# Down projection's partial sums: copied by ScalarE and added by GpSimd's accumulating DMAs, in place of VectorE's adds

## The chip, the cores and the metric

The kernel runs on one core of a Trainium2 chip. A core has TensorE (PE, matrix products into PSUM), VectorE (DVE), ScalarE (ACT), GpSimd (POOL) and SyncE (SP, which issues most DMAs); each takes its own instructions strictly in order, and they wait for one another by semaphores. The metric is the time of one execution on the device, in microseconds, and of several runs the median.

## The reference

One layer of a streaming encoder: state-space heads and latent attention heads, side by side, and then a dense SwiGLU block, for 512 prompt tokens and 64 later tokens that share the weights. The change lies in the SwiGLU block:

```python
hf = rmsnorm(x, p['norm_ffn'])
x = x + (jax.nn.silu(hf @ p['w_gate']) * (hf @ p['w_up'])) @ p['w_down']
```

`x` has 576 tokens of 1024 channels, `w_gate` and `w_up` are 1024 x 2816 and `w_down` is 2816 x 1024, all float32. In the kernel the block is followed by a norm of each token (the gain `norm_final` and the outputs `y`).

## The kernel before

The tokens lie along the free dimension: the residual `x2` is eight tiles `x2[t]` of 128 channels x 576 tokens, four of which share one buffer (`x2t[0]`, `x2t[1]`; both are called `x` in the profile). A float32 product is made of three products of rounded parts: high by high, high by low, low by high. `split_weights` makes the parts of a weight tile: ScalarE copies it into the rounded type (line 112, `wh_...`), VectorE subtracts that from the original (line 113, `wl_...`).

The hidden 2816 channels are 22 tiles `f`. For each, `gu_weights(f)` loads 2 x 512 KB of gate and up weights and forms the sums of a seven-product scheme (lines 806 to 820), and `gu_steps(f)` multiplies them in seven steps m1 to m7 into PSUM banks `ps_x`, `ps_y`, `ps_z`; some steps add onto a bank that an engine has read in between (`onto=True`). ScalarE and VectorE gather the results in `g` and `u` (lines 914 to 939), and `finish` makes `silu(g) * u` and splits it into `prod[f]` (`pr` in the profile). The tile `f = 0` has a form of its own, `gu_first`: there the norm's factor `R2` and its inverse form `Ri` (part of `fz`) are computed, and `g` is multiplied by `R2` (line 894).

The factor `R2` is put on `g` alone and left out of `u`, so that the down projection's sums lack it. In its place the residual is multiplied by `Ri`, the inverse of `R2`, once, in the first call of `down` (line 965); the norm that follows the block takes the common scale out again.

`down(fs)` is the down projection of a group of hidden tiles. The groups are `f` = 0 to 4, 5 to 9, 10 to 13, 14 to 17; the last, 18 to 21, goes through the closing code. `down` of a group is called after the first tile of the next group. For each of eight output tiles `t` and each half of the tokens (288) it makes 15 or 12 matmuls of 128 x 288 into one PSUM bank (`ps_d`; line 953), and VectorE adds the bank to the residual (line 966). Banks come from three sets in turn: `hm` has two, `sc` and `pp` three each, and `ps_x` (`sc`) and `ps_y`, `ps_z` (`pp`) use the latter two as well.

The temporaries `g`, `u` and others come from `tmp`, a ring of seven buffers of 128 x 582 floats with one tag: a new one waits until what last read its buffer is done.

The closing code multiplies the last group in two parts of the tokens (lines 953 and 1005: `add`), sums the squares (on ScalarE, VectorE and GpSimd), normalises and sends the output.

What order instructions take on an engine is decided in three ways. A planner orders all that isn't fixed, by a model of durations that it has. The table `ISSUE` fixes, for each engine, a sequence of instructions by their number in the order in which the code makes them; it covers the whole of the first part of the kernel and, with its last lines, some instructions of the SwiGLU block. And the closing part is written in its order by hand (`manual_schedule`).

Of the kernel before, what the change touches and what calls it, by code (L numbers as in the profile page):

```python
# [14 lines left out]
ALU = mybir.AluOpType  # L15
# [39 lines left out]
def hybrid_layer_kernel(ctx: ExitStack, tc: tile.TileContext, a, o):  # L55
    nc = tc.nc
    pe, act, dve, pool, sp = nc.tensor, nc.scalar, nc.vector, nc.gpsimd, nc.sync
# [58 lines left out]
    def weights(src, n, name):  # L116

        raw = wslot(wpool, f"wr_{name}")
        sp.dma_start(raw[:, :n], src)
        return split_weights(raw[:, :n], name)  # L120
# [12 lines left out]
    def wk(w, k, m=P):  # L133
        return tuple(z[:, k * m : (k + 1) * m] for z in w)
# [30 lines left out]
    def norm_steps(R, src, n, view=lambda z: z, eps=True):  # L165

        w = R.shape[1] if len(R.shape) == 2 else T
        y0, nv, u = (view(tmp(f"nr_{z}", w)) for z in "yvu")

        def first():  # L170
            act.activation(y0, src, AF.Ln, scale=1.0 / n, bias=epsb if eps else 0.0)
            dve.tensor_scalar(nv, src, -0.5 / n, -0.5 * EPS if eps else 0.0, ALU.mult, ALU.add)
            act.activation(y0, y0, AF.Exp, scale=-0.5)
            act.activation(u, y0, AF.Square)

        def second():
            dve.tensor_tensor(u, u, nv, ALU.mult)
            dve.scalar_tensor_tensor(R, u, 1.5, y0, ALU.add, ALU.mult)

        return first, second, nv  # L180
# [115 lines left out]
    for hf in range(2):  # L296
        cols = slice(hf * TH, (hf + 1) * TH)
# [441 lines left out]
    cat_y, x2, x2t = [], [], []  # L739
# [117 lines left out]
    def fbank(tag, name):  # L857
        return bank(tag, name)[:, :TH]
# [87 lines left out]
    def down_terms(fs, t):  # L946
        w = weights(a["w_down"][t][:, fs[0] * P : (fs[-1] + 1) * P], len(fs) * P, f"d{fs[0]}_{t}")
        return [(wk(w, k), prod[f]) for k, f in enumerate(fs)]

    def down_half(ps, terms, cols, first=True, last=True):  # L950
        for k, ((whi, wlo), (xhi, xlo)) in enumerate(terms):
            for i, (w, x) in enumerate(((whi, xhi), (whi, xlo), (wlo, xhi))):
                pe.matmul(  # L953
                    ps, w, x[:, cols], start=first and k == 0 and i == 0, stop=last and k == len(terms) - 1 and i == 2,
                )

    def down(fs):

        for t in range(KT):
            terms = down_terms(fs, t)  # L960
            for hf, cols in enumerate(HC):
                ps = fbank(("hm", "sc", "pp")[(2 * t + hf) % 3], f"ps_d{fs[0]}_{t}")
                down_half(ps, terms, cols)
                if fs[0] == 0:
                    dve.tensor_tensor(x2[t][:, cols], x2[t][:, cols], Ri[:, cols], ALU.mult)
                dve.tensor_tensor(x2[t][:, cols], ps, x2[t][:, cols], ALU.add)  # L966

    CUTS = (0, 5, 10, 14, LAST, FT)
    PARTS = tuple(range(i, j) for i, j in zip(CUTS, CUTS[1:]))
# [2 lines left out]
    for part in PARTS:  # L972
        for f in part:
            if f:
                first, rest, middle = gu_steps(f)
                for step in (first, *late, *middle):
                    step()
                late = rest
            if f == part[0] and f:
                for step in late:  # L980
                    step()
                late = ()
                down(prev)
        prev = part
# [15 lines left out]
    def lbank(tag, name, i):  # L1000
        return bank(tag, name)[:, : parts[i].stop - parts[i].start]
# [30 lines left out]
    ps = [lbank(tag, f"ps_l0_{t}", 0) for t, tag in enumerate(("hm", "hm", "sc", "pp"))]  # L1032
# [36 lines left out]
    with tc.manual_schedule(engines={pe.engine, dve.engine, pool.engine, act.engine}):  # L1069
        pn0, pn1 = lbank("sc", "ps_n3_0", 0), bank("pp", "ps_n3_1")[:, : len(BL)]  # L1070
        first, second, _ = norm_steps(pn0, pn0, D, eps=False)
# [32 lines left out]
        first, second, _ = norm_steps(Rt, pn1, D, eps=False)  # L1104
# [32 lines left out]
def issue_in_order(tc, nc):  # L1137
# [48 lines left out]
405 395 391 396 398 394 392 400 399 401 403 402 420 406 404 408 407 409 412 410 417 414 411 413 418 462 416 421 423  # L1186
419 464 425 422 424 415 433 431 426 432 429 428 427 438 430 434 469 463 436 435 437 439 442 441 443 466 440 444 451
465 446 467-468 452-453 445 447 455 454 448 473 475 456 477 476 474 457 472 470 478 458 449 479 488 459 490 485 492
480 489 491 471 450 503 481 505 493-494 482 460 495 487 500 507 504 496 506 518 461 508 502 510 568 575 545 509 512
483 525 511 497 520 519 501 522 486 484 573 521 515 513 517 548 523-524 570 498 530 537-538 527 543 516 526 565 499  # L1190
542 528 555 540 560 514 529 532 553 547 552 557 533 562 541 539 534 550 577 558 531 563 579 578 544 580 535
""",
    "ACT": """
0-5 8 6-7 10 9 13 11 14 12 15 17-18 16 21 19 24 20 23 40 22 25 44 26-27 51 28-33 48-49 55 34-35 37 36 59 50 41-42
# [6 lines left out]
230 237 236 271 231 244 235 247 238 245 248-251 246 256 254 260 253 261 255 258 262 257 264 252 266 265 263 267-268  # L1201
277 269 259 272-276 283 279-281 284 286 282 278 292 285 290 287 289 288 301 291 293 295 294 297 299 296 300 302-303
298 308 304-305 309 306 311 328 307 310 315-316 312-314 329 317 330 318-319 331 335 320-324 332 336 334 333 325 337
339 338 344-345 342 346 343 326 347-348 353-355 352 351 327 356-357 362 340 363 360 358 341 361 364-366 349 373-374
350 359 375 370 367 369 368 376-378 371 379-380
""",
    "POOL": """
0-3 7 18 28 4 8 5 9 6 10 26 11 27 12 29 13-17 20-23 19 24-25 31 30 32-42 53 55 57 59 54 56 58 60 43-52 61-73
""",
    "SP": """  # L1210
11-14 16 15 17-20 23 22 25 21 24 31 26 32 39-40 36 33 38 41-42 37 43-47 55 77 62 79 54 56 58 63 81 57 60 59 61 68 66
# [102 lines left out]
```

## Time and profile before

| what | us |
|---|---|
| median of 3 runs | 654.88 (653.42 to 655.2) |
| span of the profiled execution, first to last instruction | 651.7 |
| matmuls of the four down projections ahead of the closing code (line 953, `ps_d`) | 314.5 to 581.9 |
| last gate and up matmul onto `ps_x` (line 852) | 618.2 |
| the 64 adds of line 966 | 327.5 to 583.3 |
| VectorE busy in the whole span | 512.4 |
| ScalarE busy in the whole span | 339.3 |

The profile counts instructions and busy time of each engine. A matmul of 128 x 288 is listed with some 0.295 us because it overlaps the next; their number in a stretch tells the pace. "Idle before" is time in which an engine stood still ahead of an instruction, with what ended it. In a timeline, the columns are the start, the duration, the engine, the line, the operation, what is written from what, and the number of like instructions that were merged.

### The profile page before, as it was taken

The numbers are of one execution on the slowest core, as the hardware profiler recorded it, in microseconds if no ns is written. First come the engines' busy times: TensorE is split into PE (matmuls) and PEld (weight loads), VectorE is DVE, ScalarE is ACT, GpSimd is POOL, SyncE is SP. The second block draws the span as 40 slices with busy tenths as digits, with TensorE's granted clock in tenths as the row PEclk, the third lists the DMA queues.
The fourth block names the chain that finished last, engine by engine and source line by source line (L and its number), as shares of the span: only waits on it lengthen the run. The fifth ranks groups of instructions, "written<-read, shape, count | busy, mean of one in ns | idle before, by whom it ended". The sixth has DMA issues, their size and how long they took to land.

```text
span 651.7 us, 11921 instructions
## 1 busy us (share of the span) xinstructions
PE 639.9 (98%) x4731; PEld 611.8 (94%) x4731; DVE 512.4 (79%) x935; ACT 339.3 (52%) x630; POOL 41.3 (6%) x80
## 2 busy tenths in 40 slices
PE   9999999998999999999999999999999999999995
PEld 8898989885787899999999999999999999999995
DVE  6899987899776699999996776775768577876655
ACT  7645426769674567665523445223533345334364
POOL 1321104001010000000000000000000000000023
PEclk9999999999999999999999999999999999999998
DMA  8312375323220232133422233311232224222004
GB/s 314 127 62 70 93 171 143 113 66 129 86 76 33 99 102 92 65 109 103 131 80 97 79 101 101 110 66 65 81 114 98 98 66 128 68 98 98 2 1 145
DMA packets 26151, 63.22 MB, mean 97 GB/s; under 512 B 3418, under 2 KB 10088, under 8 KB 25840
## 3 DMA queue, kind: packets, MB, share of 16 engines
q1 hardware_dynamic: 24560, 60.77, 28.3%
q0 software_dynamic: 816, 1.13, 0.8%
q8 instruction: 37, 0.61, 0.4%
q10 hardware_dynamic: 720, 0.57, 0.3%
q14 instruction: 18, 0.15, 0.1%
HBM read 58.03 MB, written 3.30 MB: 94 GB/s over the span
## 4 chain that ended last, share of the span: by engine, by line
PE 84%; DVE 3%; ACT 1%; DMA 1%; issue 1%; POOL 0%; POOLq 0%; DVEq 0%; ACTq 0%
PE ps_x L852 21%; PE ps_d L953 18%; PE ps_z L852 10%; PE ps_o L443 8%; PE ps_y L852 5%; PE ps_in L128 4%; PE ps_z L443 3%; PE ps_l L953 3%; PE ps_p L852 2%; PE sc L657 2%; PE pv L704 1%; PE ptp L679 1%; PE ps_v L590 1%; PE ps_q L443 1%; PE ps_y L527 1%
## 5 line engine op out<-in xcount | busy, mean ns | idle before, releaser
L953 PE MATMUL ps_d<-pr,wh_d 128*128 128x288 f32 x576 | 115.4, 294 | 0.0
L852 PE MATMUL ps_x<-xop,wh_gu_S 128*128 128x288 f32 x504 | 101.8, 295 | 0.0
L953 PEld LDWEIGHTS ps_d<-pr,wh_d 128*128 128x128 f32 x576 | 92.5, 188 | 0.0
L953 PE MATMUL ps_d<-pr,wl_d 128*128 128x288 f32 x288 | 84.6, 295 | 0.0
L852 PEld LDWEIGHTS ps_x<-xop,wh_gu_S 128*128 128x128 f32 x504 | 80.6, 188 | 0.2
L113 DVE TENSOR_TENSOR wl_gu_S<-gu,wh_gu_S 128x1024 fp32r<-128x1024 f32 x44 | 53.6, 1224 | 34.4 <-PE ps_y L852 13.8
L852 PE MATMUL ps_x<-xop,wl_gu_S 128*128 128x288 f32 x252 | 73.4, 295 | 0.0
L112 ACT CAST wh_gu_S<-gu 128x1024 fp32r<-128x1024 f32 x44 | 46.3, 1052 | 48.4 <-PE ps_d L953 25.4
L953 PEld LDWEIGHTS ps_d<-pr,wl_d 128*128 128x128 f32 x288 | 54.0, 188 | 0.0
L852 PEld LDWEIGHTS ps_x<-xop,wl_gu_S 128*128 128x128 f32 x252 | 47.0, 188 | 0.0
L128 PE MATMUL ps_in<-xs,wh_in 128*128 128x288 f32 x256 | 45.2, 298 | 1.2 <-DVE sp_a L351 1.0
L112 ACT CAST wh_d<-wr_d 128x640 fp32r<-128x640 f32 (+1 forms) x32 | 21.5, 673 | 39.1 <-PE ps_x L852 14.8
L128 PEld LDWEIGHTS ps_in<-xs,wh_in 128*128 128x128 f32 x256 | 37.5, 188 | 2.3 <-ACT up L381 1.2
L852 PE MATMUL ps_z<-xop,gu_a 128*128 128x288 f32 x252 | 38.0, 296 | 0.0
L852 PE MATMUL ps_z<-xop,wh_gu_S 128*128 128x288 f32 x168 | 36.0, 296 | 0.0
L852 PE MATMUL ps_x<-xop,wh_gu_A 128*128 128x288 f32 x168 | 35.3, 298 | 0.0
L852 PEld LDWEIGHTS ps_z<-xop,gu_a 128*128 128x128 f32 x252 | 35.1, 188 | 0.0
L852 PE MATMUL ps_y<-xop,wh_gu_A 128*128 128x288 f32 x168 | 34.2, 294 | 0.0
L966 DVE TENSOR_TENSOR x<-ps_d,x 128x288 f32<-128x288 f32 x64 | 28.8, 453 | 6.7 <-PE ps_d L953 6.5
L112 ACT CAST wh_gu_A<-gu 128x1024 fp32r<-128x1024 f32 x22 | 23.1, 1049 | 17.5 <-PE ps_d L953 11.5
L113 DVE TENSOR_TENSOR wl_gu_A<-gu,wh_gu_A 128x1024 fp32r<-128x1024 f32 x22 | 26.9, 1223 | 5.2 <-PE ps_x L852 3.9
L1049 POOL TENSOR_TENSOR fz<-fz,sq 128x320 f32<-128x320 f32 x3 | 2.6, 880 | 445.3 <-ACT sq L1044 445.3
(339 smaller groups left out, 1643.7 us busy)
## 6 DMA issues: line engine op xcount, KB each, us to landing
gu<-in_w_gu SPq DMA_DIRECT2D x44, 512.0 KB, 3.7
wr_d<-in_w_down SPq DMA_DIRECT2D x16, 320.0 KB, 2.9
wr_in<-in_w_in SPq DMA_DIRECT2D x8, 512.0 KB, 4.0
wr_out<-in_w_out SPq DMA_DIRECT2D x8, 512.0 KB, 3.2
wr_d<-in_w_down SPq DMA_DIRECT2D x16, 256.0 KB, 2.7
cumb<-cumD SPq DMA_DIRECT2D x5, 512.0 KB, 4.6
x<-in_xT SPq DMA_DIRECT2D x2, 1152.0 KB, 7.5
wr_z<-in_w_in SPq DMA_DIRECT2D x4, 512.0 KB, 4.4
```

The source lines that it names most:

```text
L112: act.copy(hi, raw)
L113: dve.tensor_tensor(lo, raw, hi.bitcast(F32), ALU.subtract)
L128: pe.matmul(ps[:m, hf, :n], w, x[:, hf * n : (hf + 1) * n], start=start and k == 0 and i == 0, stop=stop and k == last and i == 2,)
L443: pe.matmul(ps[:, :n], w, x[:, cols], start=k == 0 and i == 0, stop=k == len(terms) - 1 and i == 2,)
L527: pe.matmul(py[64 * j : 64 * j + 64, p * P : p * P + L], xdt[:L, h * HD : (h + 1) * HD], wts[:L, h, :L], start=True, stop=True,)
L590: pe.matmul(ps[:n], l, r, start=j == 0, stop=j == 2)
L657: pe.matmul(s[:, :nk], qs[:, j, q0 : q0 + P], ks[:, j, :nk], start=True, stop=True)
L679: pe.transpose(pp[:, k : k + P], prs[p, i][:, j, b * P : b * P + P], ident)
L704: pe.matmul(pv[64 * j : 64 * j + 64, b * P :], V[b][:, h * HD : (h + 1) * HD], pts[p, b, j], start=b == 0, stop=True, skip_group_check=b > 0,)
L852: pe.matmul(ps, p, q, start=not onto and first and kp == kps[0] and j == 0, stop=onto or (last and kp == kps[-1] and j == 2), skip_group_c ...
L953: pe.matmul(ps, w, x[:, cols], start=first and k == 0 and i == 0, stop=last and k == len(terms) - 1 and i == 2,)
L966: dve.tensor_tensor(x2[t][:, cols], ps, x2[t][:, cols], ALU.add)
```

## The change

In `down`, a tile `dn` is taken from the ring of temporaries for each output tile. ScalarE copies each half of the sum from PSUM into it, and a DMA of GpSimd's queue adds `dn` to `x2[t]` with `accum_op` (128 x 576 floats, 288 KB). There are 64 copies and 32 DMAs. The multiplications by `Ri` in the first call remain on VectorE. The numbers in `ISSUE` are adapted where instructions were added or went; it no longer fixes the place of some of them.

```diff
         for t in range(KT):
             terms = down_terms(fs, t)
+            dn = tmp(f"dn{fs[0]}_{t}")
             for hf, cols in enumerate(HC):
                 ps = fbank(("hm", "sc", "pp")[(2 * t + hf) % 3], f"ps_d{fs[0]}_{t}")
                 down_half(ps, terms, cols)
                 if fs[0] == 0:
                     dve.tensor_tensor(x2[t][:, cols], x2[t][:, cols], Ri[:, cols], ALU.mult)
-                dve.tensor_tensor(x2[t][:, cols], ps, x2[t][:, cols], ALU.add)
+                act.copy(dn[:, cols], ps)
+            pool.dma_start(x2[t], dn, accum_op=ALU.add)
...
     "DVE": """
...
-480 489 491 471 450 503 481 505 493-494 482 460 495 487 500 507 504 496 506 518 461 508 502 510 568 575 545 509 512
-483 525 511 497 520 519 501 522 486 484 573 521 515 513 517 548 523-524 570 498 530 537-538 527 543 516 526 565 499
-542 528 555 540 560 514 529 532 553 547 552 557 533 562 541 539 534 550 577 558 531 563 579 578 544 580 535
+480 489 491 471 450 503 481 505 493-494 482 460 495 487 500 507 504 496 506 518 461 508 502 510 556 509 512 483 525
+511 497 520 519 501 522 486 484 559 521 515 513 517 544 523-524 498 530 537-538 527 541 516 526 499 540 528 514 529
+532 547 543 546 549 533 552 539 534 561 550 531 553 563 562 564 535
...
     "ACT": """
...
-339 338 344-345 342 346 343 326 347-348 353-355 352 351 327 356-357 362 340 363 360 358 341 361 364-366 349 373-374
-350 359 375 370 367 369 368 376-378 371 379-380
+339 338 344-345 342 346 343 326 347-348 353-355 352 351 327 356-357 362 340 363 360 358 341 361 364-366 349 373 376
+350 359 379 370 367 369 368 382 385 388 371 391 394
...
     "POOL": """
-0-3 7 18 28 4 8 5 9 6 10 26 11 27 12 29 13-17 20-23 19 24-25 31 30 32-42 53 55 57 59 54 56 58 60 43-52 61-73
+0-3 7 18 28 4 8 5 9 6 10 26 11 27 12 29 13-17 20-23 19 24-25 31 30 32-42 53 55 57 59 54 56 58 60 43-52 61-68 101-105
```

## The prediction

> **What bounds the kernel now.** I read the page first, then the chain of waits, then windows over the second half, where every line of the change lies.
>
> ```profile
> span 651.7 us, 11921 instructions
> PE 639.9 (98%) x4731; PEld 611.8 (94%) x4731; DVE 512.4 (79%) x935; ACT 339.3 (52%) x630; POOL 41.3 (6%) x80
> ...
> PE 84%; DVE 3%; ACT 1%; DMA 1%; issue 1%; POOL 0%; POOLq 0%; DVEq 0%; ACTq 0%
> ```
>
> TensorE carries 84% of the chain, VectorE 3%. But a busy PE is not yet a PE at its peak, so the windows, which count matmuls:
>
> ```profile
> core 0: us, PE busy (x) PEld busy (x) DVE busy (x) ACT busy (x) POOL busy (x), PEclk, DMA share, GB/s
> 280.00:285.00 5.00, 5.00 (x40) 5.00 (x39) 5.00 (x8) 3.25 (x6) 0.00 (x0) 1.00 0.54 188
> 285.00:290.00 5.00, 5.00 (x40) 5.00 (x39) 5.00 (x9) 4.06 (x6) 0.00 (x0) 1.00 0.00 0
> 290.00:295.00 5.00, 5.00 (x40) 5.00 (x39) 5.00 (x10) 2.22 (x5) 0.00 (x0) 1.00 0.62 206
> 295.00:300.00 5.00, 5.00 (x40) 5.00 (x39) 5.00 (x10) 1.57 (x2) 0.00 (x0) 1.00 0.19 57
> 320.00:365.00 45.00, 45.00 (x342) 45.00 (x341) 32.75 (x57) 13.97 (x20) 0.00 (x0) 1.00 0.27 94
> 410.00:450.00 40.00, 40.00 (x303) 40.00 (x303) 27.16 (x45) 12.37 (x18) 0.00 (x0) 1.00 0.22 76
> 485.00:520.00 35.00, 35.00 (x266) 35.00 (x265) 27.41 (x47) 13.03 (x18) 0.00 (x0) 1.00 0.23 83
> 550.00:585.00 35.00, 35.00 (x266) 35.00 (x265) 27.66 (x48) 13.45 (x20) 0.00 (x0) 1.00 0.28 97
> 585.00:620.00 35.00, 35.00 (x263) 35.00 (x262) 20.57 (x30) 15.27 (x22) 0.00 (x0) 1.00 0.16 55
> ```
>
> The rows from 320 to 585 hold the four down projections. Each has 7.6 matmuls a microsecond (342 in 45, 266 in 35) at a granted clock of 1.00: 0.132 us each, the same in all of them. TensorE waits for nothing there, so work taken from VectorE buys nothing. VectorE is 68 to 79% busy there, but in the four rows from 280 to 300 it has no gap at all, while TensorE still runs at full pace. Whatever VectorE gets extra in that stretch is late for somebody.
>
> **What goes from VectorE, and what ScalarE gets.** 64 adds go, 64 copies of the same shape come.
>
> ```profile
> L966 DVE TENSOR_TENSOR x<-ps_d,x x64: 447/453/458, 327.5 to 583.3; 128x288 f32<-128x288 f32 x64
> ...
> L914 ACT COPY g<-ps_x 128x288 f32<-128x288 f32 x16 | 6.4, 399 | 8.2 <-PE ps_x L852 8.2
> ```
>
> Removed: 64 x 0.453 = 29 us of VectorE, worth 0 by the rows above. Added: 64 x 0.399 = 25.5 us of ScalarE, 6.4 in each projection. Between 485 and 520 ScalarE goes from 13.0 to 19.4 busy of 35, so it keeps up. A copy ends the use of a PSUM bank. In the built program the tightest of these banks is wanted again 61 matmuls after its sum is done, 61 x 0.132 = 8.0 us, against 0.4 for the copy and about 1.05 for a weight cast ahead of it: cost 0. Without that cover each copy would cost its 0.4. The order of TensorE's instructions is the same in both built programs, and so are the distances of the weight splits from their matmuls (24 matmuls, 3.2 us, at the least after 320). Bounds here: 0 to 1 us.
>
> **The accumulating DMAs.** 32 of 288 KB, on a queue that has nothing else to do between the last head copies and the closing sums, so nothing is queued behind them there.
>
> ```profile
> q1 hardware_dynamic: 24560, 60.77, 28.3%
> ...
> qs<-rrp POOLq DMA_DIRECT2D x16, 36.0 KB, 4.4
> ...
> out_ckvT<-ckf POOLq DMA_DIRECT2D x1, 288.0 KB, 2.5
> ...
> gu<-in_w_gu SPq DMA_DIRECT2D x44, 512.0 KB, 3.7
> ```
>
> No row shows an accumulating DMA. Nearest is a plain one of the same shape and queue, 2.5 us to landing; the slowest kind on that queue took 4.4. I take 5 us as an estimate (2.5 doubled, for the second operand that is read), with 2.5 and 9.4 (5.0 plus those 4.4) as its ends. What waits: the `dn` tiles share seven buffers with `g` and `u`, and ScalarE, in order, waits for a landing before it writes a reused one. In the two later projections the copy of tile 5 waits for the DMA of tile 0, 120 matmuls = 15.8 us earlier; the waits of the next `g` and `u` come so much later that the n-th of the eight DMAs may land n x 6.9 us after the first copy at the tightest (n = 8: 420 matmuls). Behind the waiting copy stand the casts of the next gate and up weights, and TensorE behind them with 24 matmuls to spare. At 5 us: cost 0. Load on the engines: q1 moved 60.77 MB in 0.283 x 651.7 = 184 us of all sixteen, so 0.295 MB is 0.9 us and twice that 1.8, per tile of 24 matmuls (3.2 us): a share of 0.56 on top of 0.28, below 1, and weights that land in 3.7 have some 60 matmuls (8 us) between their issue and use: 0. SP's loads keep their places. At the end, the last accumulate is issued near 583 and the next read of the residual is long after:
>
> ```profile
> L1005 DVE TENSOR_TENSOR x<-ps_l,x x16: 414/454/492, 625.7 to 641.7; 128x320 f32<-128x320 f32 x8, 128x256 f32<-128x256 f32 x8
> ```
>
> 42 us for one landing: 0.
>
> The Trainium skill, "Collectives: The Full Stack", section "The bandwidth ceiling", says that an add in the DMA path reads two sources and so runs at half the rate of a copy. No run here shows it; by it the 2.5 would be at most 5.0, still 0.
>
> **The multiplications that move.** This edit isn't in the diff's words. In the built program the 16 products of the residual with `Ri` (L965, which had been spread from 299 to 330) no longer follow the adds, and seven of them stand in one burst right behind the product `g*R2` (L894). There VectorE has no gap:
>
> ```profile
> 281.29 0.75 DVE L894 TENSOR_TENSOR g<-g,R 128x576 f32<-128x576 f32 x1
> 281.96 0.69 DVE L811 TENSOR_TENSOR gu<-gu,gu 128x512 f32<-128x512 f32 x1
> ...
> 282.98 1.22 DVE L113 TENSOR_TENSOR wl_gu_A<-gu,wh_gu_A 128x1024 fp32r<-128x1024 f32 x1
> ...
> 285.31 0.69 DVE L812 TENSOR_TENSOR gu<-gu,gu 128x512 f32<-128x512 f32 x1
> ...
> 287.25 0.46 DVE L935 TENSOR_TENSOR u<-ps_z,u 128x288 f32<-128x288 f32 x1
> ...
> 288.21 2.36 DVE L113 TENSOR_TENSOR wl_gu_S<-gu,wh_gu_S 128x1024 fp32r<-128x1024 f32 x2
> ...
> 292.12 0.46 DVE L931 TENSOR_TENSOR u<-ps_x,u 128x288 f32<-128x288 f32 x1
> ...
> 298.98 1.19 DVE L965 TENSOR_TENSOR x<-x,fz 128x288 f32<-128x288 f32 x3
> ...
> 301.87 0.46 DVE L939 TENSOR_TENSOR g<-ps_x,R 128x288 f32<-128x288 f32 x1 [0.56 <-PE ps_x L852]
> ```
>
> Three in a row took 1.19, so one more costs (1.19 - 0.46) / 2 = 0.366, and seven 2.56 us. All from 281.96 to 298.98 ends 2.56 later. Who wants it, on TensorE and ScalarE:
>
> ```profile
> 285.97 0.29 PE L852 MATMUL ps_x<-xop,wl_gu_A 128*128 128x288 f32 x1
> ...
> 288.78 0.29 PE L852 MATMUL ps_z<-xop,wh_gu_S 128*128 128x288 f32 x1
> ...
> 289.05 0.43 PE L852 MATMUL ps_y<-xop,wh_gu_A 128*128 128x288 f32 x2
> ...
> 292.09 0.29 PE L852 MATMUL ps_z<-xop,wl_gu_S 128*128 128x288 f32 x1
> ...
> 293.68 0.42 PE L852 MATMUL ps_x<-xop,wh_gu_S 128*128 128x288 f32 x2
> ```
>
> ```profile
> 286.36 1.04 ACT L112 CAST wh_gu_S<-gu 128x1024 fp32r<-128x1024 f32 x1
> ```
>
> - Split `wl_gu_A`: ends 284.20, wanted 285.97: 1.77 spare, so TensorE is 0.8 late.
> - L812 feeds the cast at 286.36: the cast would begin at 288.56, end near 289.6, wanted 288.78: 0.8 to 0.9 late.
> - L935 frees a bank: 287.71, wanted 289.05: 1.34 spare, 1.2 late.
> - Second `wl_gu_S`: 290.57, wanted 292.09: 1.52 spare, 1.0 late.
> - L931 must read `ps_x` before the next product adds onto it: 292.58, wanted 293.68: 1.10 spare, 1.46 late.
>
> These overlap (TensorE's lateness from the first is part of the last's), so the largest counts: 1.5 us. At 298.98 one product stands where three stood, which gives back 0.73; at 301.87 VectorE had waited 0.56 for TensorE, so from there it follows TensorE. TensorE cannot catch up at 7.6 matmuls a microsecond. Bounds: 0 (no result was wanted so early) and 2.56 (no spare at all); 1.5 because it is read off matmul by matmul.
>
> **Sum.** 651.7 + 1.5 = 653.2 for the profiled span. The runs' median, 654.88, is 3.2 above the span of before, so 656.4.
>
> **Rivals.**
> 1. *VectorE's burst is swallowed*: 654.9, if results were used later than the rows say. Against it: five rows give a stall.
> 2. *The burst passes whole, with ScalarE's knock-on*: 2.56 and up to 1 us of late copies, about 657.6. Decides if the delayed casts push ScalarE's in-order queue beyond its gaps. Against it: gaps of ScalarE (4.06, 2.22, 1.57 busy of 5).
> 3. *The accumulating DMAs are slow, and the ring of seven buffers chokes*: slower, from 6.9 us of service each when they run one behind another. At 8 us the eighth lands 64 us after the first copy, against 420 matmuls = 55.3 and 24 more = 3.2 to spare: 5.5 us of stall, three times (after the last projection no gate and up tiles wait): 16.5, or 671. For it: 4.4 us for only 36 KB on this queue. Against it: 2.5 for 288 KB.
> 4. *Faster*, since VectorE is free: TensorE lost 3 matmuls (263 for 266) from 585 to 620, 0.4 us: 654.5 at best.
>
> The Trainium skill, "SBUF — State Buffer", section "SBUF: two separate sides", gives rival 3 a cause: a VectorE instruction in a 2-port mode keeps GpSimd from writing descriptors, and the DMA starves. By its section "Who interferes with whom" tensor_tensor has no such mode, and the rows of VectorE above are all TENSOR_TENSOR, so by the page it should not happen; no run here shows a GpSimd DMA in this stage.
>
> **How the numbers follow.** Forecast 0.50, rival 1 0.08, rival 2 0.20, rival 3 0.18, rival 4 0.04. The forecast's own range is 655.7 to 657.0. With 0.3% (2.0 us, about what a measurement of this kernel tells from no change) the bound is at 656.8, so some 0.16 of the forecast lies beyond it. Slower: 0.16 + 0.20 + 0.18 = 0.54; same: 0.34 + 0.08 = 0.42; faster 0.04. The range reaches down to 654.5 (part of rivals 1 and 4 left out) and up to 662 (rival 3 only where it just begins).
>
> **What would show it.** Right: fewer than 40 matmuls per 5 us in the windows between 283 and 295, some 11 to 12 missing in all (1.5 / 0.132), PE idle put down to VectorE's L113 and L931 (a few lines lower in the new file), then 7.6 a microsecond to the last matmuls; ScalarE near 19 of 35 in the later projections; accumulates landing in 2.5 to 9.4 us. Wrong: matmul counts that fall in the projections or right behind them, with ScalarE idle ahead of `dn` or `g` copies until a DMA lands (rival 3), or a window from 280 to 300 with no matmul missing (rival 1).

## The result, and the profile after

| | before | changed |
|---|---|---|
| median, us | 654.5 (653.42 to 655.2, 4 runs) | 657.78 (657.35 to 658.65, 4 runs) |
| ratio to before, 95% interval | | 1.0055 [1.0041, 1.0069] |
| span of the profiled execution, us | 651.7 | 655.8 |

The changed kernel is slower by 0.55%, some 3.6 us (0.0055 x 654.5); the two medians differ by 3.3 us, and the two profiled spans, unrounded 651.75 and 655.76, by 4.0. The forecast had 1.5 us. First the page of the changed kernel, its span, busy times and chain of waits:

```profile
span 655.8 us, 12044 instructions
PE 641.3 (98%) x4731; PEld 612.3 (93%) x4731; DVE 488.6 (75%) x871; ACT 360.5 (55%) x694; POOL 68.5 (10%) x112
...
PE 83%; DVE 3%; ACT 2%; issue 1%; DMA 1%; POOL 0%; POOLq 0%; ACTq 0%; DVEq 0%
```

VectorE lost 23.8 us of busy time and ScalarE gained 21.2 (less than 64 single records add up to, since neighbouring records overlap a little), and TensorE still carries the chain: relief of VectorE bought nothing. Next the windows of the changed kernel, with the columns of the prediction's windows:

```profile
core 0: us, PE busy (x) PEld busy (x) DVE busy (x) ACT busy (x) POOL busy (x), PEclk, DMA share, GB/s
280.00:285.00 5.00, 5.00 (x40) 5.00 (x39) 5.00 (x11) 1.69 (x3) 0.00 (x0) 1.00 0.61 208
285.00:290.00 5.00, 4.39 (x33) 4.15 (x32) 5.00 (x10) 4.25 (x6) 0.00 (x0) 1.00 0.00 0
290.00:295.00 5.00, 4.97 (x35) 4.51 (x34) 5.00 (x8) 2.90 (x5) 0.00 (x0) 1.00 0.29 84
295.00:300.00 5.00, 5.00 (x39) 4.91 (x38) 5.00 (x10) 2.44 (x4) 0.00 (x0) 1.00 0.34 129
...
320.00:365.00 45.00, 45.00 (x342) 45.00 (x341) 27.20 (x41) 20.37 (x37) 6.96 (x8) 1.00 0.60 144
485.00:520.00 35.00, 35.00 (x267) 35.00 (x266) 21.60 (x30) 16.86 (x32) 6.88 (x8) 1.00 0.65 153
550.00:585.00 35.00, 35.00 (x266) 35.00 (x265) 22.88 (x34) 18.11 (x35) 6.15 (x8) 1.00 0.65 156
```

From 285 to 300 there are 33, 35 and 39 matmuls where there were 40, 40 and 40: 13 are missing, 13 x 0.132 = 1.7 us. In the projections the count is what it was (342 in 45 us, 266 or 267 in 35), though the DMA engines are now busy at 0.60 to 0.65 there and not at 0.23 to 0.28. So TensorE loses once, behind the burst, and never again. The changed kernel's timeline shows how (start, duration, engine, line, operation, and in brackets an idle time with what ended it):

```profile
281.70 0.75 DVE L894 TENSOR_TENSOR g<-g,R 128x576 f32<-128x576 f32 x1
282.37 2.66 DVE L966 TENSOR_TENSOR x<-x,fz 128x288 f32<-128x288 f32 x7
...
285.92 1.21 DVE L113 TENSOR_TENSOR wl_gu_A<-gu,wh_gu_A 128x1024 fp32r<-128x1024 f32 x1
...
287.19 0.40 PE L852 MATMUL ps_x<-xop,wl_gu_A 128*128 128x288 f32 x1 [0.61 <-DVE wl_gu_A L113]
...
290.20 0.45 DVE L935 TENSOR_TENSOR u<-ps_z,u 128x288 f32<-128x288 f32 x1
...
290.70 0.53 PE L852 MATMUL ps_y<-xop,wh_gu_A 128*128 128x288 f32 x2
...
295.07 0.45 DVE L931 TENSOR_TENSOR u<-ps_x,u 128x288 f32<-128x288 f32 x1
...
295.57 0.53 PE L852 MATMUL ps_x<-xop,wh_gu_S 128*128 128x288 f32 x2
```

The seven products (x7) take 2.66 us, and TensorE starts each time within 0.1 us of the end of what it waited for: `wl_gu_A` (287.13, then 287.19), L935 (290.65, 290.70), L931 (295.52, 295.57).

All 4731 matmuls stand in both traces in one order, so the n-th of one can be held against the n-th of the other. This difference of starts, changed minus before, is 0.43 us at the matmul that began at 285.5 before, 1.99 at the one of 296, and 1.99 at every later one, to the last. The first 0.43 arose, but for 0.03, before 200 us and differs from execution to execution (more on that below). The burst cost 1.99 - 0.43 = 1.56 us.

That leaves about 2 us that no matmul shows. They lie behind the last operation of any engine. The rows of the final line of the program (its closing barrier), of the kernel before; columns: instruction and count, shortest, median and longest in ns, first and last start:

```profile
L1301 POOLq DRAIN  x3: 46/102/3489, 646.6 to 651.5; - x3
L1301 SPq DRAIN  x3: 7/7/7, 650.9 to 651.2; - x3
```

and of the changed kernel:

```profile
L1303 POOLq DRAIN  x3: 46/93/6104, 648.5 to 655.2; - x3
L1303 SPq DRAIN  x3: 7/7/7, 652.9 to 654.9; - x3
```

Each engine ends with a drain, and a barrier waits for all of them. Before, GpSimd's (POOLq) took 3.49 us from 646.56 and was done at 650.05, ahead of SyncE, which came to its own at 650.9 when the last outputs had landed. In the changed kernel GpSimd's takes 6.10 us: 648.5 + 6.1 = 654.6, while SyncE is ready at 652.9. The barrier now waits 1.75 us for GpSimd (unrounded, 654.65 - 652.90). From there to the end the two programs differ by another 0.27 us (0.84 before, 1.11 after). The whole difference: 0.43 + 1.56 + 1.75 + 0.27 = 4.0 us, all that the spans differ by; without the 0.43, which differs between executions, 3.6, as the ratio has it.

### The profile page after: what moved, and what is told of

Read it like the earlier page. It is cut to its first block, busy times and chain, and to the rows that moved or that the text cites. A ratio compares the mean times of both kernels' runs of the same rounds, so it can differ in the third digit from the quotient of the medians.

```text
span 655.8 us, 12044 instructions
## 1 busy us (share of the span) xinstructions
PE 641.3 (98%) x4731; PEld 612.3 (93%) x4731; DVE 488.6 (75%) x871; ACT 360.5 (55%) x694; POOL 68.5 (10%) x112
## 4 chain that ended last, share of the span: by engine, by line
PE 83%; DVE 3%; ACT 2%; issue 1%; DMA 1%; POOL 0%; POOLq 0%; ACTq 0%; DVEq 0%
PE ps_x L852 20%; PE ps_d L953 17%; PE ps_z L852 10%; PE ps_o L443 8%; PE ps_y L852 5%; PE ps_in L128 4%; PE ps_z L443 3%; PE ps_l L953 3%; PE sc L657 2%; PE ps_p L852 2%; PE pv L704 1%; PE ptp L679 1%; PE ps_v L590 1%; PE ps_q L443 1%; PE ps_y L527 1%
## 5 line engine op out<-in xcount | busy, mean ns | idle before, releaser
L113 DVE TENSOR_TENSOR wl_gu_S<-gu,wh_gu_S 128x1024 fp32r<-128x1024 f32 x44 | 53.5, 1221 | 50.3 <-ACT wh_gu_S L112 19.3
L968 POOL DMA_DIRECT2D x<-dn x32 | 27.6, 863 | 375.4 <-ACT dn L967 227.6
L967 ACT COPY dn<-ps_d 128x288 f32<-128x288 f32 x64 | 25.5, 398 | 32.2 <-PE ps_d L953 29.1
L113 DVE TENSOR_TENSOR wl_gu_A<-gu,wh_gu_A 128x1024 fp32r<-128x1024 f32 x22 | 26.8, 1220 | 6.5 <-PE ps_x L852 4.0
L113 DVE TENSOR_TENSOR wl_d<-wr_d,wh_d 128x640 fp32r<-128x640 f32 (+1 forms) x32 | 24.0, 753 | 9.4 <-PE ps_d L953 4.7
```

Source lines behind the costliest of these rows:

```text
L113: dve.tensor_tensor(lo, raw, hi.bitcast(F32), ALU.subtract)
L967: act.copy(dn[:, cols], ps)
L968: pool.dma_start(x2[t], dn, accum_op=ALU.add)
```

## The experiments

"Loss at the burst" is the growth of the difference of matmul starts, against the profiled execution of before, from 285.5 to 296; "closing drain" is the longest of GpSimd's drains at the closing barrier. Beside these runs the kernel before had a median of 654.67 (35 runs; for spread, burst, drain and spread_drain) and 654.72 (29 runs; for plain16 to before_drain); beside the single runs it had 654.17 (plain_sbuf) and 654.01 (burst3, burst5).

| run | median us | ratio to before | loss at the burst | closing drain |
|---|---|---|---|---|
| changed kernel | 657.78 | 1.0055 [1.0041, 1.0069] | 1.56 | 6.10 |
| spread | 656.5 | 1.0026 [1.0015, 1.0037] | 0.00 | 6.11 |
| burst | 656.07 | 1.0026 [1.0015, 1.0036] | 1.60 | 3.49 |
| drain | 656.45 | 1.0023 [1.0014, 1.0033] | 1.59 | 1.52 |
| spread_drain | 654.81 | 1.0004 [0.9992, 1.0016] | 0.00 | 1.52 |
| plain16 | 655.36 | 1.001 [0.9992, 1.0027] | -0.03 | 4.80 |
| plain32 | 656.39 | 1.0018 [1.0004, 1.0033] | -0.03 | 6.10 |
| plain64 | 659.38 | 1.0069 [1.0049, 1.009] | -0.04 | 8.71 |
| before_drain | 654.49 | 0.9996 [0.9982, 1.001] | -0.04 | 1.52 |
| plain_sbuf | one run, 657.83 | | 1.54 | 6.11 |
| burst3 | one run, 654.83 | | 0.09 | 3.49 |
| burst5 | one run, 656.5 | | 0.83 | 3.49 |

### The two terms apart

**spread**: the changed kernel, multiplications at their old places on VectorE.

```diff
-480 489 491 471 450 503 481 505 493-494 482 460 495 487 500 507 504 496 506 518 461 508 502 510 556 509 512 483 525
-511 497 520 519 501 522 486 484 559 521 515 513 517 544 523-524 498 530 537-538 527 541 516 526 499 540 528 514 529
-532 547 543 546 549 533 552 539 534 561 550 531 553 563 562 564 535
+480 489 491 471 450 503 481 505 493-494 482 460 495 487 500 507 504 496 506 518 461 508 502 510 556 560 542 509 512 483 525
+511 497 520 519 501 522 486 484 559 521 515 513 517 544 523-524 557 498 530 537-538 527 541 516 526 554 499 540 528
+548 539 551 514 529 532 547 543 546 549 533 552 534 545 561 550 531 553 563 562 564 535
```

> The changed kernel with one edit: the 16 multiplications by Ri are put back to the places on VectorE that they had before. Theory of two terms (a stall of 1.6 us behind the burst of multiplications, and a closing drain of GpSimd that ends 2.6 us later and sets the end): the stall goes, the drain stays. Span 655.8 - 1.6 = 654.2, ratio to before about 1.003, 40 matmuls in each 5 us from 285 to 300, GpSimd's closing drain still some 4.6 us beyond GpSimd's last operation. Rival A (the first term is noise between two executions, the loss lies in the DMAs or the copies): 655.8, ratio 1.0055.

The windows of this run, in the same columns:

```profile
285.00:290.00 5.00, 5.00 (x40) 5.00 (x39) 5.00 (x10) 4.42 (x7) 0.00 (x0) 1.00 0.05 19
290.00:295.00 5.00, 5.00 (x40) 5.00 (x39) 5.00 (x8) 2.11 (x2) 0.00 (x0) 1.00 0.56 167
295.00:300.00 5.00, 5.00 (x40) 5.00 (x40) 5.00 (x9) 2.44 (x4) 0.00 (x0) 1.00 0.12 46
```

40 matmuls in each again, and the ratio falls from 1.0055 to 1.0026; the drain stays. Its single span (655.1) is above the 654.2 that was expected, because this execution was 1.40 us behind before's when it came to 285, all of it from the first 200 us. Rival A falls.

**burst**: the kernel before with the multiplications at the places of the changed one, nothing else.

```diff
-465 446 467-468 452-453 445 447 455 454 448 473 475 456 477 476 474 457 472 470 478 458 449 479 488 459 490 485 492
+465 446 467-468 452-453 445 447 455 454 448 473 475 456 477 476 474 457 472 470 478 458 449 479 488 459 545 550 555 560 565 570 575 490 485 492
...
```

Here 459 is `g*R2` and the seven numbers behind it are multiplications by `Ri`; in the lines that follow, the other nine stand where the changed kernel has them.

> The kernel before with one edit: the 16 multiplications by Ri are put to the places that they have in the changed kernel, seven in a row behind g*R2; the adds stay on VectorE, no copies and no GpSimd DMAs come in. Theory of two terms: the stall of 1.6 us alone, span 651.7 + 1.6 = 653.3, ratio about 1.0025, 12 to 13 matmuls missing between 285 and 300; GpSimd's closing drain some 2.0 us beyond its last operation, as before. Rival A: 651.7, ratio 1.000.

The windows of this run:

```profile
285.00:290.00 5.00, 4.35 (x34) 4.12 (x32) 5.00 (x10) 4.20 (x5) 0.00 (x0) 1.00 0.00 2
290.00:295.00 5.00, 4.96 (x36) 4.50 (x35) 5.00 (x8) 2.95 (x5) 0.00 (x0) 1.00 0.29 79
295.00:300.00 5.00, 5.00 (x39) 4.92 (x39) 5.00 (x10) 2.44 (x4) 0.00 (x0) 1.00 0.37 134
```

11 matmuls are missing, one less than expected. 1.60 us at the burst, ratio 1.0026, closing drain 3.49 as before. The order of 16 instructions on VectorE does this alone, without a copy or an accumulating DMA.

**drain**: the changed kernel with a drain of GpSimd behind its last accumulating DMA.

```diff
     for step in late:
         step()
+    pool.drain()
     tc.keep_in_program_order(act.preload_act_table_set("natural_log_exp_and_others"))
```

> The changed kernel with one more instruction: a drain on GpSimd behind the last accumulating DMA and ahead of its first closing sum, where GpSimd has nothing else to do. Theory of two terms, with the drain's length as bookkeeping of some 0.08 us for each DMA that GpSimd issued since the start (2.6 us / 32 = 0.081): the early drain takes 4 to 5 us unseen, the closing drain ends well below 2 us after GpSimd's last operation, SP's closing sets the end again: span 655.8 - 2.1 = 653.7, ratio about 1.0025. Rival B (the closing drain waits for something of the end itself, such as the last output DMAs, or has a fixed length that the changed program got by its size): the closing drain stays at 4.6 us, span 655.8, ratio 1.0055.

The rows of the two lines that hold GpSimd's drains, the early one and those of the closing barrier:

```profile
L989 POOLq DRAIN  x1: 9052/9052/9052, 586.6 to 586.6; - x1
...
L1303 POOLq DRAIN  x3: 93/168/1515, 650.2 to 655.5; - x3
```

The closing drain is down from 6.10 to 1.52 us. The early one takes 9.05 us from 586.6, where GpSimd had nothing else to do until 630. That is longer than the 4 to 5 us that were expected. The last accumulate landed only at 593.3, so a wait for that landing may be part of it; in spread_drain, too, the early drain (8.43 us) ended 2.3 us behind the last landing. How its time divides isn't shown. The ratio falls to 1.0023: rival B falls. The single span stays at 655.9 by accident of the first 200 us (2.1 us behind before's execution at 285); the ratio over 12 runs decides.

**spread_drain**: both edits.

> The changed kernel with both edits: multiplications at their old places and the early drain. Theory of two terms, if they are all there is: 655.8 - 1.6 - 2.1 = 652.1, ratio 1.000 to 1.001. If copies or accumulating DMAs cost something of their own on the path, it is left here: each 0.001 of the ratio is 0.65 us. Rival A with B: 655.8.

1.0004 [0.9992, 1.0016]. With the two terms gone, 64 copies on ScalarE and 32 accumulating DMAs cost nothing that can be measured; in the trace the difference of matmul starts stays within 0.01 us of 0.54 from 285 us to the last matmul. Each term is seen twice, and they add up: 0.0026 (burst) + 0.0026 (what spread leaves) against 0.0055.

### What the drain counts

**plain16, plain32, plain64**: the kernel before with N plain DMAs of 2 KB on GpSimd's queue.

```diff
+    scr = dpool.tile([P, 4 * N], F32, name="scr")
+    for j in range(N):
+        pool.dma_start(scr[:, 4 * j : 4 * j + 4], ident[:, 4 * (j % 32) : 4 * (j % 32) + 4])
     tc.keep_in_program_order(act.preload_act_table_set("natural_log_exp_and_others"))
```

> The kernel before and, besides, 16 plain DMAs of GpSimd's queue, 2 KB each, from the identity tile to a scratch tensor that nobody reads; they wait for nothing of the SwiGLU block and are issued behind the head copies, long before the end. Theory (the closing drain takes some 0.081 us for each DMA that GpSimd issued since the start; before has 24 of them and a drain of 2.05 us beyond GpSimd's last operation): 2.05 + 16 x 0.081 = 3.35 us; it would end 0.4 us behind SP's closing, so span 651.7 + 0.4 = 652.1, ratio near 1.0005, hardly to be told from 1. Rival C (the drain grows with bytes or with accumulation, not with the count; these move 32 KB in all): 2.05 us, ratio 1.000.

> As the run with 16, with 32 plain DMAs of 2 KB, as many as the change issues accumulating ones. Theory by count: closing drain 2.05 + 32 x 0.081 = 4.65 us beyond GpSimd's last operation, as in the changed kernel; the end is 1.7 us later (2.0 with the small step behind the clearing of the semaphores), ratio 1.0026 to 1.003. Rival C: 2.05 us, ratio 1.000.

> As the run with 16, with 64 plain DMAs of 2 KB. Theory by count: closing drain 2.05 + 64 x 0.081 = 7.2 us, end 4.3 us later (4.6 with the small step), ratio 1.0065 to 1.007. Rival C: 2.05 us, ratio 1.000. Rival D (the drain has a ceiling, as if only some of the DMAs were kept): the same 4.65 us as with 32.

**before_drain**: the kernel before with the early drain.

> The kernel before with an early drain on GpSimd, behind its 24 DMAs and ahead of its first closing sum. Theory by count: the early drain takes some 2 us unseen, the closing one less than 0.2 us beyond GpSimd's last operation; SP's closing sets the end as it did before, so span 651.7 and ratio 1.000. If a drain had a price of its own here, the ratio would show it.

The closing line's row in each of these four, in this order, and for the last its early drain and GpSimd's last two operations:

```profile
L1302 POOLq DRAIN  x3: 46/102/4799, 647.4 to 652.7; - x3
```

```profile
L1302 POOLq DRAIN  x3: 46/102/6104, 647.5 to 654.1; - x3
```

```profile
L1302 POOLq DRAIN  x3: 46/102/8714, 648.8 to 658.1; - x3
```

```profile
L1301 POOLq DRAIN  x3: 34/102/1515, 647.3 to 652.3; - x3
...
L987 POOLq DRAIN  x1: 4865/4865/4865, 182.5 to 182.5; - x1
...
647.37 1.41 POOL L1017 TENSOR_TENSOR x<-x,R 128x256 f32<-128x256 f32 x2 [4.40 <-ACT R L1121]
```

With no DMA issued since the last drain the closing one takes 1.515 us, all but 0.07 of it beside GpSimd's last two multiplications (to 648.78). Each DMA that GpSimd issued since the last drain adds 0.082 us to it: (3.489 - 1.515) / 24 = 0.082 for the 24 that the kernel before has, (4.799 - 3.489) / 16 = 0.082, (6.104 - 3.489) / 32 = 0.082, (8.714 - 3.489) / 64 = 0.082. The 32 plain DMAs of 2 KB, all issued by 201 us, give the same 6.104 us as the change's 32 accumulating ones of 288 KB. It is the count; rivals C and D fall. The early drain of before_drain missed its expectation: 4.87 us and not some 2, directly behind its last DMAs, the last of which landed at 186.3, 1.0 us before the drain's end. In time, plain64 is slower by 0.69% (6 runs) and before_drain unchanged. plain32's 1.0018 is below the 1.0026 expected, which its interval holds.

### The accumulating DMAs by themselves

**plain_sbuf**: the changed kernel, DMAs without the addition. The down projections' sums replace the residual.

```diff
-            pool.dma_start(x2[t], dn, accum_op=ALU.add)
+            pool.dma_start(x2[t], dn)
```

> The changed kernel with its 32 DMAs of GpSimd's queue as plain copies of dn over the residual tile, without the addition (so the down projections' sums replace the residual and the output is another one); same tiles, order and count. If it is the addition that takes the 4.7 us from issue to landing of the accumulating ones, the plain ones land in 2.5 to 3 us, as the one plain DMA of 288 KB of that queue did (2.5), and the DMA share from 485 to 520 falls from 0.65 to about 0.5. If the loads of weights beside them or the way from SBUF to SBUF take it: 4.7 us again. The span does not change either way: 655.8 but for what differs between executions, with the closing drain at 4.66 us, since the count is the same.

The DMA rows of the changed kernel (queue: packets, MB, share of the 16 engines; GpSimd's time for an issue, shortest, median and longest in ns; issue: KB each, median us to landing):

```profile
q0 software_dynamic: 5424, 10.57, 9.1%
...
L968 POOL DMA_DIRECT2D x<-dn x32: 852/862/925, 330.5 to 584.9; - x32
...
x<-dn POOLq DMA_DIRECT2D x32, 288.0 KB, 4.7
```

and of this run:

```profile
q0 software_dynamic: 3376, 10.57, 4.6%
...
L968 POOL DMA_DIRECT2D x<-dn x32: 546/546/580, 330.9 to 585.2; - x32
...
x<-dn POOLq DMA_DIRECT2D x32, 288.0 KB, 2.5
```

The same bytes between the same tiles take half the engines' time and 2.5 us without the addition, 4.7 with it; 0.3 us of that lies in the issue itself (0.86 against 0.55). From 485 to 520 the DMA share falls from 0.65 to 0.45, where 0.5 was expected. So the price is the addition's, not that of the way or of the loads beside it. Loss at the burst (1.54) and drain (6.11) are those of the changed kernel: the slower DMA was hidden.

### How much lateness the spare time swallows

**burst3, burst5**: the kernel before, with three and with five of the multiplications moved behind `g*R2`.

```diff
-465 446 467-468 452-453 445 447 455 454 448 473 475 456 477 476 474 457 472 470 478 458 449 479 488 459 490 485 492
+465 446 467-468 452-453 445 447 455 454 448 473 475 456 477 476 474 457 472 470 478 458 449 479 488 459 545 550 555 490 485 492
...
```

(with five, 560 and 565 follow 555)

> The kernel before with three of the multiplications by Ri, not seven, moved behind g*R2 (the others at their old places). Theory of the prediction's sum (each costs VectorE 0.366 us, and the tightest of the later results, L931, has 1.10 us to spare): 3 x 0.366 = 1.10 us late, all of it inside the spare time, so TensorE loses 0 us between 285 and 296. Rival E (what hurts is that TensorE's supply is late at all, in proportion to the burst: 1.6 / 7 each): 0.7 us.

> As the run with three, with five moved: 5 x 0.366 = 1.83 us late, less 1.10 to spare = 0.7 us lost between 285 and 296. Rival E: 1.1 us.

The burst itself, in the timelines of the two:

```profile
283.26 1.19 DVE L965 TENSOR_TENSOR x<-x,fz 128x288 f32<-128x288 f32 x3
```

```profile
284.05 1.93 DVE L965 TENSOR_TENSOR x<-x,fz 128x288 f32<-128x288 f32 x5
```

Lost: 0.09 us with three, 0.83 with five, 1.60 with seven. The theory had 0, 0.73 and 1.46; rival E 0.7 and 1.1 for the first two. These are single runs, but each loss is read within a trace. The loss begins where n x 0.37 us passes the 1.1 us that L931 has to spare, and then grows with the full price of each product.

## Why the prediction was right or wrong

**The burst: right, to the tenth.** Forecast 1.5 us, from 1.46 at L931; measured 1.56, 1.60 and 1.59 in the changed kernel, burst and drain. The very row was right too: at the product behind L931 TensorE is at 295.57 in place of 293.68, 1.89 later, and 1.89 - 0.43 = 1.46. That it never catches up was right: the difference of starts is the same at the last matmul as at 296. Foreseen were 11 to 12 missing matmuls, 13 are. Of the two idle times of TensorE that were to show it, only the one behind L113 is listed (0.61 us); the lateness behind L931 shows in the starts alone.

**What goes and comes on VectorE and ScalarE: right.** The 64 adds of 0.45 us taken from VectorE were worth 0. The 64 copies took 25.5 us, and their row in the changed kernel (busy, mean ns, then the idle time ahead of them and what ended it) shows that ScalarE waited for TensorE's sums, never for a landing:

```profile
L967 ACT COPY dn<-ps_d 128x288 f32<-128x288 f32 x64 | 25.5, 398 | 32.2 <-PE ps_d L953 29.1 <-ACT dn L967 2.3 <-ACT wh_gu_A L112 0.6
```

ScalarE was busy 16.9 and 18.1 of 35 us in the two later projections, not 19.

**The accumulating DMAs on their way: right.** 5 us was the estimate, 4.7 the median (3.3 to 6.6). What the Trainium skill says in "Collectives: The Full Stack", section "The bandwidth ceiling", of a collective's adding step, two reads at half the rate, agrees with the trace here: 2.5 against 4.7 us and 4.6% against 9.1%. spread_drain bounds what they and the copies cost on the path: not more than 0.0016 x 654.7 = 1 us.

**The tail: this step failed.** The prediction put "42 us for one landing: 0" on the end of the accumulates. It asked only who reads the residual next. It did not ask what the issue of a DMA leaves behind on the engine that issued it, so this term is missing from its sum. 32 more DMAs lengthen GpSimd's closing drain by 32 x 0.082 = 2.6 us. Of these SyncE's own closing hid 0.87 (650.91 against 650.05), so 1.75 us came out at the end, more than the burst. The row that could have warned was in the trace of before: a drain of 3.49 us on GpSimd, done only 0.9 us ahead of the last waiter. Small as it was, it was the second of the two chains that end the program, and the change added to it.

**The sum.** 651.7 + 1.5 lacked 1.75 + 0.27. The 3.2 "above the span" holds as a difference of two numbers, but it isn't a fixed cost of a run: runs last only 1.7 to 2.1 us longer than their own spans (655.8 and 657.46 in the changed kernel). The rest is that the profiled execution of before was quicker than most: 66 other runs of before have spans from 650.8 to 655.0, median 652.8, and every other trace is 0.4 to 2.3 us behind it by 200 us, ahead of all that the change touches.

**Luck.** The kernel became slower, as forecast, but less than half of the 3.6 us came from the step that the prediction had worked out. The median of 657.78 lies beyond the forecast's own 655.7 to 657.0. The wider range holds it only because that was drawn up to 662 for rivals 2 and 3, neither of which occurred. The burst by itself makes 0.26% (run burst), less than the 0.3% by which the prediction tells slower from the same. Its chances hold a slip besides: of the forecast's range of 1.3 us, 0.2 lie beyond 656.8, a share of about 0.16. Of a chance of 0.50 that is 0.08, but the sum takes 0.16. With 0.08, slower had 0.46 and the same 0.50.

**The rivals.** Rival 2 names 657.6, near what came, but by another way: the burst did not pass whole (1.56 of 2.66 us), and TensorE lost nothing to a late copy. Rival 1 fell with the 1.56 us. Rival 3 did not occur; the landings (4.7 us, 6.6 at most) kept inside 6.9. Nor did the cause for it that the Trainium skill names in "SBUF — State Buffer", section "SBUF: two separate sides". Its section "Who interferes with whom" gives tensor_tensor no such mode, and the trace agrees: GpSimd took 0.85 to 0.93 us for each of the 32 issues, beside a VectorE that was busy for 23 of 35 us. Rival 4 did not occur either: the difference of starts is still 1.99 us at the last matmul, so nothing was won back behind the projections.

## What to carry to other kernels

A DMA moved to GpSimd's queue has a cost at the end of the program besides those on its way: see when each engine's closing drain is done, as for any other chain that ends late. Where such DMAs are many, a drain on GpSimd at a place where it idles moves that cost out of sight; where they are few, it may be hidden already. And when an edit loosens an order, look for where the freed instructions gather: they cost nothing until their sum passes the smallest spare time behind them, and from there their full price.

## What the runs showed of the hardware

- GpSimd's closing drain takes 0.082 us for each DMA that GpSimd has issued since its last drain, whether 2 KB or 288 KB, plain or accumulating, landed by 202 or at 590 us (24, 40, 56 and 88 DMAs: 3.49, 4.80, 6.10 and 8.71 us, 1.52 with none). A drain close behind the DMAs takes longer: 4.87 us behind 24, 8.43 and 9.05 behind 56. The Trainium skill, "VectorE: DVE Perf Modes", section "The DRAIN you can't avoid", knows two kinds of drain, one behind each VectorE operation and one that the runtime puts ahead of and behind a program, about 12 ns on all engines. The closing drains here stand on the kernel's own last line; SyncE's 7 ns would fit the second kind; GpSimd's long one fits neither.
- The step of 0.27 us between the barrier and the end is a pause of GpSimd between its last drain and the next instruction, 0.36 us where the kernel before has 0.04. In drain and spread_drain it lies one instruction earlier, and the step is 0.43 us. It isn't there in plain16 and plain32 and is in plain64, so the accumulating DMAs alone don't explain it; the cause stays open.
- Ahead of 180 us all these programs do the same, yet TensorE's start of the same matmul differs by up to 2.3 us between their executions. Single spans can't tell terms of 1 to 2 us apart; the growth of the difference over the changed stretch can (1.54 to 1.60 in the four programs with the whole burst, -0.04 to 0.00 in those without).
